# Token-major linear layers: four chunks of 256 columns, one token tile at a time, become chunks of 512 columns over all token tiles at once

## The chip, the cores and the metric

One core of a Trainium2 chip runs the whole program. Its engines are TensorE (PE, with its weight loads shown as PEld), VectorE (DVE), ScalarE (ACT), GpSimd (POOL) and SyncE (SP, which issues most DMAs). PE writes its results to PSUM, here eight banks of 128x512 float32. The metric is the device time of one execution in microseconds (us); the lower the better.

## What is computed

Two transformer blocks on 512 tokens of width 1024, batch 1, in float32. What matters here are four linear layers whose output is wanted token by token (tokens on the partitions):

```
z = h @ w_in                        # mixer A: v columns (512) of [u, gate, q, k, v, f]
z = h @ w_in                        # mixer B: v columns (512) of the dilated heads, 128 of the sliding heads
k, v = split(mem_n @ w_kv, 2)       # cross attention, in both layers: v, 256 memory tokens x 1024
... = h @ gdn_w_in                  # gated delta net: output gate z, 1024 columns; out = norm(o) * silu(z)
```

All other linear layers are wanted feature by feature and are not touched.

## The kernel before, in words

**Precision and pieces.** A float32 product is made of three fp32r matmuls (`mm3`): high x high, high x low, low x high part. Activations come as pairs `(high, low)` of tiles `xs[k]`, one for each of eight blocks k of 128 features. Weights come in pieces of 128x1024: a DMA into `ws`, a cast on ACT to `wh` (line 130), a subtraction on DVE for `wl` (line 131). `BUFS` gives 4 buffers to `ws` and 3 each to `wh` and `wl`. `wap` returns a generator over a chunk's pieces, so that a piece is asked for only when the loop comes to it.

**Token-major layers.** `lin_t` goes over chunks of 256 columns. For a chunk it takes the whole list of pieces (two, of four k each), and then for each tile of 128 tokens `lin_1` takes one PSUM bank of tag `lin`, runs 8 x 3 matmuls with the tokens as the stationary operand and 256 columns of weights moving (lines 152 to 154), and calls the evacuation. `lin_f` is the feature-major counterpart: weights stationary, 512 tokens moving.

**PSUM.** `BANKS = {"lin": 2, "pt": 1, "s": 3, "o": 2}`: eight banks with a tag each. `s` serves attention scores, the LRU's gates (lines 487, 488), and in the gated delta net (GDN) the decay matrices (lines 980 to 983), the transposes of X (line 1034), and in each level of the block inverse the products `pz` (line 1055), `px` (line 1062) and `py` (line 1065). DVE writes Z out of `pz` (line 1059), then subtracts `py` from Y (line 1067) and `px` from X (line 1069).

**Order.** The kernel is written with a library that places the instructions itself: a planner goes through them with the order of writing as their priority and its own estimates of durations. Whatever is ready and first in the order goes next into its engine's queue, so that later work fills an engine that would otherwise stand still. A tile takes a buffer of its tag when its first instruction is placed, and gives it back after its last reader. The queues are fixed when the kernel is built; on the chip each engine runs its queue in order and waits on semaphores.

**The sum of squares.** `rms_prep` makes the squares (ACT, line 202) and adds them on POOL (line 207). The rest, matmuls with ones (line 222), a reciprocal root on DVE (lines 224 to 242) and its broadcast (lines 251 to 254), is written at the first call of `rms()`, in most layers in the first evacuation.

**The sites.** In `ab` (evacuation line 381) the v layer stands before the LRU. In `cd` (line 545) it is the first layer, and its evacuation is the first to call `rms()`. In `xa_kv` (lines 657, 658: ACT writes the high part, DVE the low part) there are two tiles of tokens; the feature-major K layer stands before it. In `gdn` the z layer stands after four groups of two heads (lines 869, 870) and before the gating of all heads (lines 876 to 887): `sz` and the pairs `gy` take buffers of tag `x` (16), which `xs` and the groups' tiles hold until they are through.

Of the kernel before, what the change touches and what calls it, by code (L numbers as in the profile page):

```python
# [11 lines left out]
AF = mybir.ActivationFunctionType  # L12
OP = mybir.AluOpType
# [5 lines left out]
S = 512  # L19
D = 1024  # L20
NT = 4
# [12 lines left out]
class Kern:  # L34
# [129 lines left out]
    def lin_t(self, w, chunks, xs, evac, cols=256, N=S):  # L164

        for c in chunks:
            ws = list(w(c))
            for t in range(N // 128):
                self.lin_1(ws, t, xs, lambda p: evac(c, t, p), cols)

    def lin_1(self, ws, t, xs, evac, cols=256):
        p = self.psum("lin")[:, :cols]
# [192 lines left out]
    def ab(self):  # L365
        nc, A = self.nc, self.A
        V = VCOL
        vec = self.vec
        xs, rms = self.rms_prep(self.hT, V["ab_norm"])
        w = self.wap("ab_w", 8, 128)  # L370
        ahead = lambda c: self.early.pop(0) if self.early else w(c)
        fx, c = self.t("fx")[:8], self.t("c")[:8]
        u, g = self.tiles("u", 4), []
        v = self.tiles("v", 4, "x")
# [3 lines left out]
            nc.vector.tensor_tensor(y, p, rms()[1], op=OP.mult)  # L378

        def ev_v(c, t, p):  # L380
            nc.scalar.activation(v[t][:, c * 256:(c + 1) * 256], p, AF.Copy, scale=rms()[0][:, t:t + 1])

        self.lin_f(ahead, [0], xs, lambda n, p: nc.vector.tensor_tensor(fx, p, rms()[1][:8], op=OP.mult), cols=8)

# [9 lines left out]
        lw = self.tconst("lruw")  # L394
        self.lruw, self.lruw2 = lw[:, :S], lw[:, S:]
        uc = self.conv4(u, V["conv_w"], V["conv_b"])
        self.lin_t(self.wap("ab_wv", 8, 256), range(2), xs, ev_v)
        self.lru(uc)
        g += self.tiles("g", 4)
        self.lin_f(w, range(12, 16), xs, ev)  # L400
# [123 lines left out]
    def cd(self):  # L524
        nc, V = self.nc, VCOL
        xs, rms = self.rms_prep(self.hT, V["cd_norm"])
        C, Sn = self.pair("CS")
        w = self.wap("cd_w", 8, 128)

        def rotated(p, scale):  # L530
            z, zr, y = self.t("z"), self.t("zr"), self.t("qk")
            nc.scalar.activation(z, p, AF.Copy, scale=scale)
            for a, b in ((0, 32), (32, 0), (64, 96), (96, 64)):
                nc.sync.dma_start(zr[a:a + 32], z[b:b + 32])
            nc.gpsimd.tensor_tensor(zr, zr, Sn, op=OP.mult)
            nc.vector.tensor_tensor(z, z, C, op=OP.mult)
            nc.vector.tensor_tensor(y, z, zr, op=OP.add)
            return y

        v = self.tiles("v", 4, "x")  # L540
        vd_ = self.t("vd")
        vd = [vd_[:, t * 128:(t + 1) * 128] for t in range(NT)]

        def ev_v(c, t, p):
            nc.scalar.activation(v[t][:, c * 256:(c + 1) * 256] if c < 2 else vd[t], p, AF.Copy, scale=rms()[0][:, t:t + 1])

        self.lin_t(self.wap("cd_wv", 8, 256), range(2), xs, ev_v)
        self.lin_t(self.wap("cd_wvd", 8, 128, -2), [2], xs, ev_v, cols=128)
        nc.vector.tensor_tensor(C, self.cos, rms()[1], op=OP.mult)
        nc.vector.tensor_tensor(Sn, self.sin, rms()[1], op=OP.mult)  # L550
        ys = [self.pair("y", "y", F32R) for _ in range(4)]
        qp, kp = [None] * 8, [None] * 5

        def proj_q(i, n):
            def ev(n, p):
                qp[i] = self.q_parts(rotated(p, -0.125))
            self.lin_f(w, [n], xs, ev)

        def proj_k(i, n):
            def ev(n, p):  # L560
                kp[i] = self.k_parts(rotated(p, 1.0))
            self.lin_f(w, [n], xs, ev)

        def dilated(i):
            mn, den = self.small((128, 8), "mn"), self.small((128, 8), "den")
            o = self.psum("pt")
            for j in range(8):
                qb, e = NT - 1 - j // 2, j % 2
                h, nk, qs = 2 * i + e, (qb + 1) * 128, slice(qb * 128, (qb + 1) * 128)
                P = self.probs(self.qk(qp[i], *kp[i], e, qs, slice(0, nk)), nk, self.dstrip[:, 512 - nk:],  # L570
                               mn[:, j:j + 1], den[:, j:j + 1])
                self.pv(o[:, j * 64:(j + 1) * 64], P, nk, [v[b][:, h * 64:(h + 1) * 64] for b in range(qb + 1)])
            self.pair_out(self.o_norm(o, den, 8), ys[i])

        def sliding(i):

            mn, den = self.small((128, 8), "mn"), self.small((128, 8), "den")
            o = self.psum("pt")
            for j in range(8):
                qb, e = NT - 1 - j // 2, j % 2  # L580
                h, k0, qs = i + 4 * e, max(0, qb - 1) * 128, slice(qb * 128, (qb + 1) * 128)
                nk = (qb + 1) * 128 - k0
                P = self.probs(self.qk(qp[4 + i], *kp[4], e, qs, slice(k0, k0 + nk)), nk, self.sstrip[:, 256 - nk:],
                               mn[:, j:j + 1], den[:, j:j + 1], floor=self.nsink[:, h:h + 1])
                self.pv(o[:, j * 64:(j + 1) * 64], P, nk,
                        [vd[k0 // 128 + b][:, e * 64:e * 64 + 64] for b in range(nk // 128)])
            x = self.small((128, 8), "es")
            sinks = self.nsink.rearrange("p (e i) -> p i e", e=2)[:, i]
            nc.vector.tensor_tensor(x.rearrange("p (t e) -> p t e", e=2), mn.rearrange("p (t e) -> p t e", e=2),
                                    sinks[:, None].to_broadcast([128, NT, 2]), op=OP.subtract)  # L590
            nc.scalar.activation(x, x, AF.Exp)
            nc.vector.tensor_tensor(den, den, x, op=OP.add)
            ys.append(self.rpair("y"))
            self.pair_out(self.o_norm(o, den, 8), ys[4 + i])

        def proj(i):
            if i < 4:
                proj_k(i, 4 + i)
                proj_q(i, i)
            elif i < 8:  # L600
                if i == 4:
                    proj_k(4, 12)
                proj_q(i, 4 + i)

        proj(0)
        for i in range(8):
            proj(i + 1)
            if i == 6:
                self.mem_load()
            if i == 7:  # L610
                self.xa_kv(1)
            (dilated if i < 4 else sliding)(i % 4)
        for j in range(8):
            self.dump("d_y2", rd(ys[j][0]), lambda o: o[j])
        self.lin_f(self.wap("cd_wo", 8, 128), range(8), ys, self.add_resid)
# [22 lines left out]
    def xa_kv(self, l):  # L638
        nc, V = self.nc, VCOL
        rcol, rbc = self.mem_r  # L640
        xs = []
        for k in range(8):
            if k % 2 == 0:
                h2, m2 = self.rpair("mx")
            c = slice((k % 2) * 256, (k % 2 + 1) * 256)
# [7 lines left out]
        vv = [[self.T("xv", "y", F32R) for _ in range(2)] for _ in range(2)]  # L653

        def ev_v(c, t, p):
            (h, m), r, c = vv[t], rcol[:, t:t + 1], slice(c * 256, (c + 1) * 256)
            nc.scalar.activation(h[:, c], p, AF.Copy, scale=r)
            nc.vector.scalar_tensor_tensor(m[:, c], p, r, rd(h[:, c]), op0=OP.mult, op1=OP.subtract)

        self.lin_f(self.wap("xa_wk", 8, 128, 8 * l), range(8), xs, lambda n, p: nc.vector.tensor_tensor(kT[n], p, rbc, op=OP.mult), N=256)  # L660
        self.lin_t(self.wap("xa_wv", 8, 256, 4 * l), range(4), xs, ev_v, N=256)
        self.xkv = (kT, vv)

    def xa(self, l):
# [121 lines left out]
    def gdn(self):  # L786
# [76 lines left out]
        sz = []  # L863

        def ev_z(c, t, p):
            if t == 0:
                sz.append(self.T("sz", "x").rearrange("p (n i c) -> p n i c", n=NT, i=2))
            th, z = self.t("zt", tag="P")[:, :256], sz[c].rearrange("p n i c -> p n (i c)")[:, t]
            nc.scalar.activation(th, p, AF.Tanh, scale=hr[:, t:t + 1])
            nc.vector.scalar_tensor_tensor(z, th, 1.0, p, op0=OP.add, op1=OP.mult)  # L870

        self.lin_t(self.wap("gdn_wz", 8, 256), range(4), xs, ev_z)
        ys = self.ys = [self.rpair("gy") for _ in range(8)]
        for grp in range(4):
            o, rs = ot[grp]
# [1030 lines left out]
def chunks(w, cols):  # L1906

    k, n = w.shape
    return np.ascontiguousarray(w.reshape(k // 128, 128, n // cols, cols).transpose(2, 1, 0, 3)).reshape(n // cols, 128, -1)


def layout(I):
    f = np.float32
    A = {}
# [17 lines left out]
    w = I["ab_w_in"][0]  # L1932
    u, g, q, k, v, fl = np.split(w, [512, 1024, 1536, 2048, 2560], axis=1)
    A["ab_w"] = chunks(np.concatenate([u, q, k, g], 1), 128)
    A["ab_wv"] = chunks(v, 256)
    A["ab_wf"] = chunks(fl, 8)
    A["ab_wo"] = chunks(I["ab_w_out"][0], 128)
    bd = np.zeros((2, 4, 128, 128), f)
# [6 lines left out]
    qc, kc, vc, qd, kd, vd = np.split(w, [512, 1024, 1536, 2048, 2176], axis=1)  # L1945
    qd = qd.reshape(D, 2, 4, 64).transpose(0, 2, 1, 3).reshape(D, 512)
    A["cd_w"] = chunks(np.concatenate([qc, kc, qd, kd], 1), 128)
    A["cd_wv"] = chunks(vc, 256)
    A["cd_wvd"] = chunks(vd, 128)
    wo = I["cd_w_out"][0]  # L1950
    A["cd_wo"] = chunks(np.concatenate([wo[:512], wo[512:].reshape(2, 4, 64, D).transpose(1, 0, 2, 3).reshape(512, D)]), 128)
    A["sink"] = np.ascontiguousarray(I["cd_sink"].reshape(1, 8))
    A["xa_wq"] = np.concatenate([chunks(I["xa_w_q"][l], 128) for l in range(2)])
    A["xa_wk"] = np.concatenate([chunks(I["xa_w_kv"][l][:, :D], 128) for l in range(2)])
    A["xa_wv"] = np.concatenate([chunks(I["xa_w_kv"][l][:, D:], 256) for l in range(2)])
    A["xa_wo"] = np.concatenate([chunks(I["xa_w_o"][l], 128) for l in range(2)])
    A["mlp_wu"] = np.concatenate([chunks(I["mlp_w_up"][l], 128) for l in range(2)])
    A["mlp_wd"] = np.concatenate([chunks(I["mlp_w_down"][l][g * 1024:(g + 1) * 1024], 128) for l in range(2) for g in range(4)])
# [14 lines left out]
    w = I["gdn_w_in_2"][0]  # L1973
    q, k, v, z = (w[:, i * 1024:(i + 1) * 1024] for i in range(4))
    A["gdn_w"] = chunks(np.concatenate([x[:, g * 256:(g + 1) * 256] for g in range(4) for x in (k, q, v)], 1), 128)
    A["gdn_wz"] = chunks(z, 256)
    A["gdn_wab"] = chunks(w[:, 4096:], 16)
    A["gdn_conv"] = I["gdn_conv_w_2"][0].reshape(4, 24, 128).transpose(2, 1, 0).reshape(128, 96)
    A["gdn_dt"], A["gdn_alog"], A["gdn_nw"] = I["gdn_dt_bias_2"], I["gdn_a_log_2"], I["gdn_norm_w_2"].reshape(128, 1)
# [63 lines left out]
```

## Time and profile before

| | |
|---|---|
| median of 3 runs | 2798.21 us (2798.03 to 2803.38) |
| the profiled execution's own time | 2798.65 us |
| its span in the trace | 2796.9 us |
| PE, PEld busy | 2682.8 us (96%), 2294.2 us (82%) |
| DVE, ACT, POOL busy | 1770.3 us (63%), 1367.6 us (49%), 181.9 us (7%) |
| DMA | 332.58 MB, mean 119 GB/s |

The span is what the trace covers; the time of the execution is a little longer. Busy shares are of the span. Matmuls overlap in PE's pipeline, so a matmul's duration in the trace is longer than the distance to the next one's start. The five places that are touched lie at about 50 to 79 us (`ab`), 223 to 246 (cross attention of layer 0), 757 to 785 (`cd`), 963 to 986 (cross attention of layer 1) and 1741 to 1837 (GDN).

### The profile page before, as it was taken

To read this page: it belongs to the slowest core of one execution; us is meant where nothing else is said; L and a number is where in the kernel's file an instruction comes from. 1 tells how busy PE (TensorE), PEld (TensorE's weight loads), DVE (VectorE), ACT (ScalarE), POOL (GpSimd) and SP (SyncE) were. 2 spreads that over 40 slices of the span, in tenths; PEclk is the share of its full clock that TensorE was granted. 3 is DMA by queue.
4 is the path that set the end of the run, shared out by engine and by line. 5 is a ranking of instruction groups with operands and counts; after the bars stand their busy time and mean duration, and the time that the engine had idled before them with its cause. 6 is when DMAs were issued, how large, how long until landed. Compare 5 with 4: busy or idle time off the path is not lost. (4 is left out here: it accounts for less than half of the span.)

```text
span 2796.9 us, 40163 instructions
## 1 busy us (share of the span) xinstructions
PE 2682.8 (96%) x15128; PEld 2294.2 (82%) x15128; DVE 1770.3 (63%) x3583; ACT 1367.6 (49%) x2541; POOL 181.9 (7%) x185
## 2 busy tenths in 40 slices
PE   8999999999999999999999999997997999997996
PEld 6889888888888888888887788997886888897885
DVE  6775564443447656535445877567878367667878
ACT  5654443332346544423334644335885255534885
POOL 1101010000111010100002000000001001000001
PEclk9999999999999999999999999998999999998998
DMA  4314233333333331334433222323887212013985
GB/s 138 100 41 148 70 94 92 97 98 98 91 86 92 106 106 42 109 98 127 149 94 128 85 71 63 93 69 129 303 291 275 91 42 73 24 45 100 313 295 190
DMA packets 122534, 332.58 MB, mean 119 GB/s; under 512 B 21716, under 2 KB 37748, under 8 KB 122328
## 3 DMA queue, kind: packets, MB, share of 16 engines
q1 hardware_dynamic: 119896, 321.43, 36.4%
q0 software_dynamic: 2432, 8.46, 0.8%
q8 instruction: 123, 2.02, 0.3%
q14 instruction: 83, 0.68, 0.1%
HBM read 301.49 MB, written 28.02 MB: 118 GB/s over the span
## 5 line engine op out<-in xcount | busy, mean ns | idle before, releaser
L130 ACT ACTIVATE wh<-ws 128x1024 fp32r<-128x1024 f32 (+2 forms) x521 | 534.1, 1030 | 828.8 <-PE lin L153 594.8
L131 DVE TENSOR_TENSOR wl<-ws,wh 128x1024 fp32r<-128x1024 f32 (+2 forms) x521 | 616.6, 1192 | 154.8 <-ACT wh L130 152.5
L152 PE MATMUL lin<-xs,wh 128*128 128x512 f32 (+2 forms) x1080 | 428.3, 397 | 7.4 <-ACT xs L197 5.9
L153 PE MATMUL lin<-xs,wh 128*128 128x512 f32 (+2 forms) x1080 | 429.0, 397 | 2.6 <-DVE xs L198 2.4
L154 PE MATMUL lin<-xs,wl 128*128 128x512 f32 (+2 forms) x1080 | 427.7, 396 | 0.9 <-DVE wl L131 0.9
L152 PEld LDWEIGHTS lin<-xs,wh 128*128 128x128 f32 (+2 forms) x1080 | 202.9, 188 | 50.9 <-ACT xs L197 6.8
L153 PEld LDWEIGHTS lin<-xs,wh 128*128 128x128 f32 (+2 forms) x1080 | 203.0, 188 | 47.6 <-DVE xs L198 7.1
L154 PEld LDWEIGHTS lin<-xs,wl 128*128 128x128 f32 (+2 forms) x1080 | 203.0, 188 | 42.3 <-DVE wl L131 1.4
L347 DVE TENSOR_TENSOR h<-lin,h 128x512 f32<-128x512 f32 x112 | 77.4, 691 | 247.6 <-PE lin L154 247.5
L152 PE MATMUL lin<-sr,wh 128*128 128x512 f32 x512 | 199.2, 389 | 0.0
L153 PE MATMUL lin<-sr,wh 128*128 128x512 f32 x512 | 199.2, 389 | 0.0
L154 PE MATMUL lin<-sr,wl 128*128 128x512 f32 x512 | 199.2, 389 | 0.0
L734 DVE SCALAR_TENSOR_TENSOR ra<-lin,bc 128x512 f32<-128x512 f32 x64 | 44.3, 692 | 168.5 <-PE lin L154 165.9
L305 ACT ACTIVATE P<-s,mn 128x256 f32<-128x256 f32 (+1 forms) x224 | 114.3, 514 | 52.7 <-DVE mn L303 50.1
L1539 PE MATMUL o<-oh,Rh 128*128 128x256 f32 x512 | 131.1, 292 | 5.6 <-PEq L1382 2.2
L1539 PE MATMUL o<-oh,Rl 128*128 128x256 f32 x512 | 130.0, 290 | 0.0
L152 PEld LDWEIGHTS lin<-sr,wh 128*128 128x128 f32 x512 | 96.1, 188 | 20.1
L154 PEld LDWEIGHTS lin<-sr,wl 128*128 128x128 f32 x512 | 96.1, 188 | 19.9
L153 PEld LDWEIGHTS lin<-sr,wh 128*128 128x128 f32 x512 | 96.1, 188 | 19.8
L153 PE MATMUL s<-wl,exh 128*128 128x512 f32 x256 | 105.1, 410 | 5.3 <-DVE wl L131 5.1
L313 PE MATMUL o<-c_ident,P 128*128 128x128 f32 x536 | 97.0, 282 | 12.2 <-ACT P L305 11.4
L1539 PEld LDWEIGHTS o<-oh,Rh 128*128 128x128 f32 x512 | 101.7, 199 | 8.6 <-ACT ex L1555 4.1
(605 smaller groups left out, 6174.4 us busy)
## 6 DMA issues: line engine op xcount, KB each, us to landing
ws<-in_moe_wgu SPq DMA_DIRECT2D x128, 512.0 KB, 5.9
ws<-in_mlp_wu SPq DMA_DIRECT2D x64, 512.0 KB, 3.6
ws<-in_mlp_wd SPq DMA_DIRECT2D x64, 512.0 KB, 3.6
ws<-in_moe_wd SPq DMA_DIRECT2D x64, 512.0 KB, 5.6
yd<-ey SPq DMA_DIRECT2D x56, 256.0 KB, 4.7
ws<-in_gdn_w SPq DMA_DIRECT2D x24, 512.0 KB, 3.7
ws<-in_ab_w SPq DMA_DIRECT2D x16, 512.0 KB, 4.4
ws<-in_xa_wk SPq DMA_DIRECT2D x16, 512.0 KB, 3.7
```

Of the source, the lines that this page charges most:

```text
L130: nc.scalar.activation(wh, ws, AF.Copy)
L131: nc.vector.tensor_tensor(wl, ws, rd(wh), op=OP.subtract)
L152: mm(out, a[0], b[0], start=start, stop=False)
L153: mm(out, a[0], b[1], start=False, stop=False)
L154: mm(out, a[1], b[0], start=False, stop=stop)
L305: nc.scalar.activation(P[:, :nk], p[:, :nk], AF.Exp, bias=mn, scale=-1.0, accum_out=den)
L313: nc.tensor.transpose(pt[:, b * 128:(b + 1) * 128], P[:, b * 128:(b + 1) * 128], self.ident)
L347: self.nc.vector.tensor_tensor(self.hT[n], p, self.hT[n], op=OP.add)
L734: nc.vector.scalar_tensor_tensor(a, p, 0.0, rms()[1], op0=OP.max, op1=OP.mult)
L1539: self.nc.tensor.matmul(p[:, j * 256:(j + 1) * 256], Rs[t][i][:, fs], oh[:, t], start=t + i == 0, stop=t == NT - 1 and i == 1)
```

## The change

A new function `lin_w` takes chunks of 512 columns. For a chunk it takes a PSUM tile for each tile of tokens, tagged `lin`, `lin`, `s`, `s` (only the first two in cross attention). It goes over the pieces of weights as they come (now two k each), and for each k over all tiles of tokens; after the last k it calls the evacuations of all tiles. Four layers call it in place of `lin_t`; the 128 columns of the sliding heads' v stay with `lin_t`. The evacuations work on 512 columns; that of z makes two `sz` tiles at a time and writes them with one DVE instruction each. The weights in DRAM are laid out in chunks of 512 columns.

```diff
+    def lin_w(self, w, chunks, xs, evac, N=S):
+
+        for c in chunks:
+            ps = [self.psum(tag) for tag in ("lin", "lin", "s", "s")[:N // 128]]
+            for k, b in w(c):
+                for t, p in enumerate(ps):
+                    self.mm3(p, tuple(x[:, t * 128:(t + 1) * 128] for x in xs[k]), b, k == 0, k == len(xs) - 1)
+            for t, p in enumerate(ps):
+                evac(c, t, p)
 
         def ev_v(c, t, p):
-            nc.scalar.activation(v[t][:, c * 256:(c + 1) * 256], p, AF.Copy, scale=rms()[0][:, t:t + 1])
+            nc.scalar.activation(v[t], p, AF.Copy, scale=rms()[0][:, t:t + 1])
...
-        self.lin_t(self.wap("ab_wv", 8, 256), range(2), xs, ev_v)
+        self.lin_w(self.wap("ab_wv", 8, 512), range(1), xs, ev_v)
...
-        self.lin_t(self.wap("cd_wv", 8, 256), range(2), xs, ev_v)
-        self.lin_t(self.wap("cd_wvd", 8, 128, -2), [2], xs, ev_v, cols=128)
+            nc.scalar.activation(vd[t] if c else v[t], p, AF.Copy, scale=rms()[0][:, t:t + 1])
+
+        self.lin_w(self.wap("cd_wv", 8, 512), range(1), xs, ev_v)
+        self.lin_t(self.wap("cd_wvd", 8, 128, -1), [1], xs, ev_v, cols=128)
...
-            (h, m), r, c = vv[t], rcol[:, t:t + 1], slice(c * 256, (c + 1) * 256)
+            (h, m), r, c = vv[t], rcol[:, t:t + 1], slice(c * 512, (c + 1) * 512)
             nc.scalar.activation(h[:, c], p, AF.Copy, scale=r)
             nc.vector.scalar_tensor_tensor(m[:, c], p, r, rd(h[:, c]), op0=OP.mult, op1=OP.subtract)
...
-        self.lin_t(self.wap("xa_wv", 8, 256, 4 * l), range(4), xs, ev_v, N=256)
+        self.lin_w(self.wap("xa_wv", 8, 512, 2 * l), range(2), xs, ev_v, N=256)
...
         def ev_z(c, t, p):
             if t == 0:
-                sz.append(self.T("sz", "x").rearrange("p (n i c) -> p n i c", n=NT, i=2))
-            th, z = self.t("zt", tag="P")[:, :256], sz[c].rearrange("p n i c -> p n (i c)")[:, t]
+                for _ in range(2):
+                    sz.append(self.T("sz", "x").rearrange("p (n i c) -> p n i c", n=NT, i=2))
+            th = self.t("zt", tag="P")
             nc.scalar.activation(th, p, AF.Tanh, scale=hr[:, t:t + 1])
-            nc.vector.scalar_tensor_tensor(z, th, 1.0, p, op0=OP.add, op1=OP.mult)
-
-        self.lin_t(self.wap("gdn_wz", 8, 256), range(4), xs, ev_z)
+            for i in range(2):
+                z, cs = sz[2 * c + i].rearrange("p n i c -> p n (i c)")[:, t], slice(i * 256, (i + 1) * 256)
+                nc.vector.scalar_tensor_tensor(z, th[:, cs], 1.0, p[:, cs], op0=OP.add, op1=OP.mult)
+
+        self.lin_w(self.wap("gdn_wz", 8, 512), range(2), xs, ev_z)
```

## Rows read from the trace of the kernel before

**Rows 1.** The page, part 1: busy us (share of the span) xinstructions of each engine.

```profile
PE 2682.8 (96%) x15128; PEld 2294.2 (82%) x15128; DVE 1770.3 (63%) x3583; ACT 1367.6 (49%) x2541; POOL 181.9 (7%) x185
```

**Rows 2.** Timeline of PE, cd: start us, us, engine, line, op, out<-in, shapes, count.

```profile
769.81 0.28 PE L152 MATMUL lin<-wh,xs 128*128 128x256 f32 x1
...
781.93 0.28 PE L154 MATMUL lin<-wh,xs 128*128 128x256 f32 x1
```

**Rows 3.** Timeline of PE, a feature-major layer of 512 columns.

```profile
399.61 0.39 PE L153 MATMUL lin<-y,wh 128*128 128x512 f32 x1
...
406.64 0.39 PE L154 MATMUL lin<-y,wl 128*128 128x512 f32 x1
```

**Rows 4.** Windows, cd and cross attention: stretch, length, each engine's busy us, PEclk, DMA.

```profile
757.00:797.00 40.00, 38.50 (x316) 37.58 (x315) 11.97 (x27) 12.91 (x21) 2.80 (x3) 1.00 0.23 70
960.00:990.00 30.00, 30.00 (x254) 29.82 (x253) 18.10 (x27) 16.11 (x26) 0.00 (x0) 1.00 0.58 175
```

**Rows 5.** Windows, instructions of tile xs alone: PE, PEld, DVE, ACT busy (count), PEclk.

```profile
1741.60:1769.60 28.00, 10.05 (x63) 8.12 (x63) 0.00 (x0) 0.00 (x0) 1.00 0.15 40
1769.60:1787.90 18.30, 15.95 (x131) 15.77 (x131) 0.00 (x0) 0.00 (x0) 1.00 0.34 97
1787.90:1797.60 9.70, 3.92 (x17) 3.42 (x17) 0.00 (x0) 0.00 (x0) 0.65 0.65 207
1797.60:1836.60 39.00, 25.89 (x174) 22.20 (x174) 0.00 (x0) 0.00 (x0) 1.00 0.25 82
```

**Rows 6.** Timeline of PE, GDN's last group; in brackets idle time before and its releaser.

```profile
1787.97 1.09 PE L1034 MATMUL s<-c_ident,X 128*128 128x128 f32 x8 [2.40 <-DMA X<-x]
...
1795.60 2.17 PE L1062 MATMUL s<-X,Z 128*128 128x64 f32 x16
1797.60 1.95 PE L1065 MATMUL s<-Z,X 128*128 128x64 f32 x16
...
1809.94 1.14 PE L1049 MATMUL s<-X,Z 64*64 64x64 f32 x16
```

**Rows 7.** Timeline of PE, the start of cd.

```profile
757.59 0.28 PE L152 MATMUL lin<-wh,xs 128*128 128x256 f32 x1
...
761.77 1.05 PE L222 MATMUL pt<-ones,ssq 128*128 128x1 f32 x8 [1.26 <-POOL ssq L207]
...
765.67 0.68 PE L252 MATMUL pt<-dg,ones 128*128 128x128 f32 x4 [0.23 <-DVE dg L251]
```

**Rows 8.** Timeline of DVE, the start of cd.

```profile
762.86 0.16 DVE L224 TENSOR_SCALAR ms<-pt 128x4 f32<-128x4 f32 x1 [2.26 <-PE pt L222]
...
765.04 0.16 DVE L242 SCALAR_TENSOR_TENSOR b<-u,b 128x4 f32<-128x4 f32 x1
```

**Rows 9.** Windows, GDN after the wait for X: all engines' busy us, PEclk, DMA.

```profile
1788.00:1796.00 8.00, 8.00 (x44) 8.00 (x44) 3.04 (x5) 0.60 (x1) 0.00 (x0) 0.58 0.64 192
```

**Rows 10.** Timeline of all engines, cross attention: a tile of tokens ends and is evacuated.

```profile
965.94 0.28 PE L154 MATMUL lin<-wh,mx 128*128 128x256 f32 x1
...
966.26 0.47 ACT L657 ACTIVATE xv<-lin,mem 128x256 fp32r<-128x256 f32 x1 [1.94 <-PE lin L154]
...
966.77 0.49 DVE L658 SCALAR_TENSOR_TENSOR xv<-lin,mem,xv 128x256 fp32r<-128x256 f32 x1 [1.19 <-ACT xv L657]
```

**Rows 11.** Groups by shape: count | busy us, mean ns of one | idle before.

```profile
L886 ACT ACTIVATE gy<-o,gdn_nw 128x512 fp32r<-128x512 f32 x8 | 5.4, 688 | 4.8 <-PE o L885 4.6
...
L1422 DVE SCALAR_TENSOR_TENSOR z<-yg,wh,z 128x512 f32<-128x512 f32 x16 | 11.1, 739 | 0.0
```

**Rows 12.** Timeline of DVE, GDN's last group.

```profile
1800.25 0.68 DVE L1069 TENSOR_TENSOR X<-X,s 128x512 f32<-128x512 f32 x1
...
1835.32 0.17 DVE L876 TENSOR_TENSOR b<-b,rcol 128x8 f32<-128x8 f32 x1
```

More of the change, by code (lines that the diff above doesn't have):

```diff
@@ L544, in ev_v @@
         def ev_v(c, t, p):
-            nc.scalar.activation(v[t][:, c * 256:(c + 1) * 256] if c < 2 else vd[t], p, AF.Copy, scale=rms()[0][:, t:t + 1])
-        self.lin_t(self.wap("cd_wv", 8, 256), range(2), xs, ev_v)
-        self.lin_t(self.wap("cd_wvd", 8, 128, -2), [2], xs, ev_v, cols=128)
+            nc.scalar.activation(vd[t] if c else v[t], p, AF.Copy, scale=rms()[0][:, t:t + 1])
+        self.lin_w(self.wap("cd_wv", 8, 512), range(1), xs, ev_v)
+        self.lin_t(self.wap("cd_wvd", 8, 128, -1), [1], xs, ev_v, cols=128)
         nc.vector.tensor_tensor(C, self.cos, rms()[1], op=OP.mult)
@@ L1934, in layout @@
     A["ab_w"] = chunks(np.concatenate([u, q, k, g], 1), 128)
-    A["ab_wv"] = chunks(v, 256)
+    A["ab_wv"] = chunks(v, 512)
     A["ab_wf"] = chunks(fl, 8)
@@ L1947, in layout @@
     A["cd_w"] = chunks(np.concatenate([qc, kc, qd, kd], 1), 128)
-    A["cd_wv"] = chunks(vc, 256)
+    A["cd_wv"] = chunks(vc, 512)
     A["cd_wvd"] = chunks(vd, 128)
@@ L1954, in layout @@
     A["xa_wk"] = np.concatenate([chunks(I["xa_w_kv"][l][:, :D], 128) for l in range(2)])
-    A["xa_wv"] = np.concatenate([chunks(I["xa_w_kv"][l][:, D:], 256) for l in range(2)])
+    A["xa_wv"] = np.concatenate([chunks(I["xa_w_kv"][l][:, D:], 512) for l in range(2)])
     A["xa_wo"] = np.concatenate([chunks(I["xa_w_o"][l], 128) for l in range(2)])
@@ L1975, in layout @@
     A["gdn_w"] = chunks(np.concatenate([x[:, g * 256:(g + 1) * 256] for g in range(4) for x in (k, q, v)], 1), 128)
-    A["gdn_wz"] = chunks(z, 256)
+    A["gdn_wz"] = chunks(z, 512)
     A["gdn_wab"] = chunks(w[:, 4096:], 16)
```

## The prediction

> **What bounds the kernel now.** I read the page's busy times first: TensorE (PE) is busy 96% of the span [rows 1], so a gap on PE is nearly always lost time, and 1% of PE work is worth about as much time. Then I looked at how fast PE runs its two kinds of matmul. In the layers that the change touches, 102 matmuls of 256 columns start 12.12 us apart from first to last, 0.1200 us each [rows 2]. In the layers of 512 columns, 32 start over 7.03 us, 0.2268 us each [rows 3]. So a 512-column matmul is 0.0132 us cheaper than two of 256. Last I looked at each of the five call sites for what keeps PE busy and what it waits for. In the V projection of cross attention PE has no gap at all; at the start of `cd` it is busy 38.5 of 40 us [rows 4]; in the gated delta net (GDN) the z projection fills the holes of a long chain [rows 5, 6].
>
> **Removed: half the matmuls, and their overhead.** The counts follow from the loops (three matmuls per tile of tokens, k and chunk). `ab_wv`: 2 chunks x 4 tiles x 8 x 3 = 192 of 256 columns; `cd_wv`: 192; `xa_wv`: two layers of 4 x 2 x 24 = 192 each; `gdn_wz`: 4 x 4 x 24 = 384. Together 1152 become 576 of 512 columns: 576 x 0.0132 = 7.6 us less PE work (1.3 in `ab`, 1.3 in `cd`, 2.5 in both cross attentions, 2.5 in GDN). Pieces of weights stay 128x1024, so their DMAs, their casts and their number are the same, at the same rate.
> The rows leave 13 ns of overhead on each matmul beyond its columns at 2.4 GHz. The Trainium skill (TensorE: Matmul & The Clock Gate, Back-to-back issue gap) gives columns/2.4 + 2.5 ns for an isolated pair of matmuls; by it the pair would save 2.5 ns, estimated 1.4 us in all. The rows measure five times that, and I use them.
>
> **ab.** The v chunk holds two of the three `s` banks for some 22 us, and the LRU's matmuls need two at a time. They are not on the path: their result is needed only after attention. The next user of `lin` finds its bank: tile 0 ends 9 matmuls (2.0 us) before the chunk does, and its evacuation takes about 0.7. So -1.3 us.
>
> **cd: the sum of squares comes later.** `rms()` runs its PE and DVE work when an evacuation first asks for it. Before, that was after tile 0's 24 matmuls: PE waited 1.26 us for the last `ssq` and ran L222, and while DVE made the reciprocal root, from 762.86 to 765.2, PE ran on with tile 1 [rows 7, 8]. After, the first evacuation stands behind all 96 matmuls of the chunk. All four accumulators are then full, none can be emptied before the root is there, and the next layer needs a `lin` bank. What covered the DVE chain is gone: PE is idle from L222's end (762.82 in the old times) to L252 at 765.67, 2.85 us [rows 7]. Gained are the old stalls, 1.26 + 0.23 [rows 7], since 84 matmuls (19 us) can run before the eighth k is needed.
> The idle time has a second price. After the one gap of 2.4 us in GDN the granted clock read 0.58 (a mix of its two levels) over the next 8 us [rows 6, 9]: 8 x 0.42 = 3.4 us of PE time; after the 1.26 us in `cd` it stayed at 1.00 [rows 4]. 2.85 is nearer the first, so I take 3.4 (bounds 0 and 3.4). `cd`: -1.3 - 1.5 + 2.85 + 3.4 = +3.5 us.
>
> **Cross attention: both lin banks at once.** With two tiles of tokens the chunk takes both `lin` banks, and its tiles end only three matmuls apart. Before, one bank emptied while the other filled: ACT starts 0.04 us after a tile's last matmul ends, DVE 0.04 after ACT [rows 10], and PE never waited [rows 4]. After, ACT and DVE work on 512 columns, 0.69 and 0.74 us by the like instructions [rows 11]. Tile 0's last matmul runs 0.39 us from its start [rows 3], so its bank is free 0.39 + 0.04 + 0.69 + 0.04 + 0.74 + 0.05 = 1.95 us after that start, where PE wants it 4 x 0.227 = 0.91 us after. That is 1.04 us of idle PE, once between the two chunks and once before the layer that follows, in two layers: 4.2 us. In layer 1 a few steps of the last sliding head can fill, so I take 3.2 (bounds 0, if other work always fills, and 4.2, or 1 us more each if a cast stands in front). Net -2.5 + 3.2 = +0.7.
> The Trainium skill (Perfetto Trace Analysis, Matmuls) says independent groups should rotate through different banks so that emptying one overlaps the next group's matmuls; that speaks against this loop, and the sum above is its price here.
>
> **GDN: the filler takes banks that the chain needs.** This is the large term. Before, z needs only `lin`, which the chain of group 3 doesn't use. The planner places single matmuls of z wherever PE would stand still: 62 of the 384 before 1769.6 (the row has 63, one is group 3's last), 131 up to 1787.9 while the block inverse goes through DRAM, 17 up to 1797.6, and 174 more up to 1836.6 [rows 5]. After, tiles 2 and 3 of each chunk sit in two of the three `s` banks until the chunk is done and evacuated. The inverse's levels need a bank for `px` and another for `py` at once: L1069 empties `px` only after L1065 has read X and written `py`. With one bank left `py` waits for the end of the z chunk.
> How long? z is 192 x 0.2268 = 43.5 us. Up to the arrival of X PE has run 193 x 0.120 = 23.2 us of it, and I let it do as much after; if one `s` bank slows group 3's decay stage, z gains on PE what the chain loses. So 20.3 us are left, the second chunk, with its banks taken. Some 2.0 more run before L1065 [rows 5]. Then the remaining 18.3 us run in one stretch while the chain stands, plus 1.0 for the evacuation of a bank and 0.9 for Y's two halves through one bank: `py` is 20.2 us late. From L1065 (1797.60) to the last scale (L876, 1835.32) [rows 6, 12] the chain takes its own time, with no z to fill it. It gives back 1.3 us, as z no longer ends at 1836.6, behind the chain, and some PE work of afterwards can move into the gaps: z's end frees the `x` slots for six of eight heads' gating, 24 transposes and 36 matmuls of the first two output tiles, about 2.2 + 4.3 = 6.5 us. Net +12.4 us, its own 2.5 of saved matmuls included. Bounds: -2.5, if the chain always gets its banks, and +20, if nothing moves in.
>
> **Sum.** -1.3 + 3.5 + 0.7 + 12.4 = +15.3 us on the profiled execution's 2798.65 (span 2796.9): 2813.9, and the median of the runs shown lies 0.4 below that execution: **2813.5 us**, slower by 0.5%.
>
> **Rivals.** A measurement of this kernel can tell about 0.2% (5.6 us) from no change.
> (1) Faster: the work of filling is placed around the chain, so that GDN keeps its -2.5, and the sum of squares is placed inside `cd`'s chunk, where PE has the operand since 761.7. Then -7.6 - 1.5 + 3.2 = -5.9, 2792.3 us (2789 if the cross attention's waits are filled as well). For it: the planner already mixes single matmuls finely. Against it: in `cd` L222 stood behind tile 0's matmuls, in the order of writing, and while `py` is blocked z is the only work that is ready. It decides if `py` is under 3 us late. Chance 0.15.
> (2) No change: `py` finds its bank, the rest as above: -1.3 + 3.5 + 0.7 - 2.5 = +0.4, 2798.6. It holds if the z chunk is nearly through when X arrives, or takes its `s` banks late. Chance 0.24.
> (3) Slower by another way: banks of a tag are given out in the order of writing. Then z's tiles 2 and 3 wait for the last `px` of group 3 (L1049, 1809.94) [rows 6]; until then only tiles 0 and 1 run, through three pieces of weights, 36 matmuls or 8.2 us. 35.3 us of z are left, where before 143 x 0.12 = 17.2 were: +18, in all +21, 2819. Chance 0.11.
> My forecast (`py` blocked, 2803 to 2823 with the bounds of its terms): 0.50.
>
> **Chances and range.** Faster 0.15, same 0.25, slower 0.60. The likeliest time is 2813. For 8 in 10 the range must reach over rival (2) and the edge of rival (1) below and over rival (3) and a second loss of clock above: 2794 to 2828.
>
> **What would show it.** In the new trace: 512-column matmuls of `wh,xs` starting every 0.227 us; in `cd` L222 after 96 matmuls, a gap of about 2.9 us after it and a clock below 1 behind that; between the two `xa_wv` chunks gaps of about 1 us that end on L658; in GDN an L1062 followed by a run of z matmuls, then L1065 some 20 us later than before, and PE gaps up to the last scale. The forecast is wrong if L1065 follows L1062 at once, if L222 sits inside the chunk, or if the PE gaps at those four places add up to less than 8 us.

## The result: 44 us slower, and where the time went

The changed kernel takes 2842.26 us (median of 4 runs, 2841.41 to 2848.9) against 2798.12 for the kernel before (4 runs, 2796.59 to 2803.38): a ratio of 1.0168, with a 95% interval of 1.0151 to 1.0184. Slower was forecast, by a third of this. The page of the changed kernel, busy times and granted clock by slices:

```profile
PE 2706.7 (95%) x14552; PEld 2289.7 (81%) x14552; DVE 1770.4 (62%) x3575; ACT 1360.9 (48%) x2517; POOL 181.9 (6%) x185
...
PEclk9999999999989999999999999698999999998998
```

PE has 576 matmuls fewer than in [rows 1] and is busy 23.9 us longer. Wider matmuls cannot do that; the clock line tells how: its slice 26 of 40 reads 6, and the mean granted clock fell from 0.982 to 0.968.

To find the places I matched the same instruction in both traces and took the difference of its starts (us; the last column names such pairs, before and after). In this kernel's numbering lines stand 10 or 11 lower down behind `lin_w` (L207 is now L217, L222 is now L232), 12 or 13 in GDN (L1034 is now L1047, the last px L1049 is now L1062), and up to 4 lower still in the experiments.

| stretch | forecast | measured | starts before, after |
|---|---|---|---|
| ab | -1.3 | +0.5 | 222.89, 223.39 |
| V layer, cross attention 0 | +0.8 | +1.2 | 252.08, 253.82 |
| start of cd | +3.5 | +12.9 | 752.15, 753.83 and 838.06, 852.62 |
| rest of cd, V layer 1 | -0.1 | +1.8 | 1038.07, 1054.43 |
| GDN's second group | 0 | +3.0 | 1655.82, 1672.31 and 1692.18, 1711.69 |
| GDN's last group with z | +12.4 | +24.2 | 1767.16, 1787.41 and 1862.08, 1906.52 |
| everything else | 0 | +0.4 | spans 2796.9, 2840.9 |

The 0.8 and -0.1 are the forecast's +0.7 split over the two layers. Two rows hold more than their layer. Of ab's +0.5, -0.6 lies ahead of the layer, in the start of the kernel, where nothing was changed: from the pair at 49.49 (48.89 after) to the pair at 104.18 (104.90), with the V layer and the LRU between them, ab costs +1.3. And V layer 1 by itself, from 963.06 (980.47) to 999.99 (1016.35), comes out 1.05 below the kernel before; the +2.85 ahead of it is the rest of cd, 1.5 of it beside a granted clock of 0.50 from 949.7 to 960.0, where the kernel before had 0.50 for 3.4 us.

**GDN.** PE's timeline of the last group after the change:

```profile
1789.52 0.47 PE L154 MATMUL lin<-wh,xs 128*128 128x512 f32 x1
1804.01 1.97 PE L1047 MATMUL s<-c_ident,X 128*128 128x128 f32 x8 [14.01 <-DMA X<-x]
...
1833.35 1.96 PE L1062 MATMUL s<-X,Z 64*64 64x64 f32 x16 [0.68 <-ACT Z L1059]
1835.24 0.79 PE L152 MATMUL s<-wh,xs 128*128 128x512 f32 x1
...
1882.76 0.39 PE L152 MATMUL lin<-wh,gy 128*128 128x256 f32 x1 [0.38 <-ACT gy L899]
```

and windows over it (stretch, length, busy time and count of PE, PEld, DVE, ACT, POOL, granted clock, DMA):

```profile
1780.00:1788.00 8.00, 8.00 (x55) 6.93 (x54) 4.84 (x15) 3.94 (x16) 0.00 (x0) 1.00 0.22 66
1788.00:1796.00 8.00, 2.00 (x11) 1.29 (x9) 5.80 (x24) 1.24 (x6) 0.00 (x0) 0.80 0.09 8
1796.00:1804.00 8.00, 0.00 (x0) 0.00 (x0) 1.32 (x2) 0.00 (x0) 0.00 (x0) 0.50 0.41 118
1804.00:1812.00 8.00, 7.14 (x32) 6.66 (x32) 1.38 (x2) 0.60 (x1) 0.00 (x0) 0.50 0.23 89
...
1836.00:1844.00 8.00, 8.00 (x40) 6.84 (x38) 2.35 (x8) 2.34 (x8) 0.00 (x0) 0.71 0.01 3
```

z starts with its tiles 0 and 1, in `lin`. After 36 matmuls, three pieces of weights times 12, nothing more of it runs, and PE stands 14.01 us for X, where the kernel before stood 2.40 [rows 6]. No `s<-wh,xs`, which is z's tiles 2 and 3, starts before 1835.24, right behind the last px, although from a matmul at 1783.04 up to X's arrival at 1804.01 nothing is written to an `s` bank. Nor is the chain's `py` (L1078) blocked: it starts at 1813.86, right behind `px` (L1075, 1810.40). So it is rival (3), not the forecast: z does not take the chain's banks, it waits behind the chain for them. The difference of 24 us in its parts: X comes 16.0 us later, against a lag of 20.2 at the pair where the table's stretch begins (-4.2). From X to the last px the chain takes 29.34 us instead of 21.97, at a clock of 0.50 (+7.4). From there to the first matmul of the output projection (`lin<-wh,gy`, 1882.76; 1838.86 before) it is 49.4 us instead of 28.9 (+20.5): 156 matmuls of z are left, 156 x 0.2268 = 35.4 us, where 143 x 0.120 = 17.2 were (+18.2), and the clock of 0.71 from 1836 to 1844 is worth about the other 2.3 (an estimate, 8 x 0.29); the missing 0.5 comes behind that matmul.

**cd.** PE behind the v chunk, and DVE in the gap:

```profile
781.20 0.95 PE L232 MATMUL pt<-ones,ssq 128*128 128x1 f32 x8
786.01 1.19 PE L262 MATMUL pt<-dg,ones 128*128 128x128 f32 x4 [3.86 <-DVE dg L261]
```

```profile
783.18 0.16 DVE L252 SCALAR_TENSOR_TENSOR b<-u,b 128x4 f32<-128x4 f32 x1
783.26 1.22 DVE L131 TENSOR_TENSOR wl<-ws,wh 128x1024 fp32r<-128x1024 f32 x1
784.40 0.15 DVE L250 TENSOR_TENSOR u<-b 128x4 f32<-128x4 f32 x1
```

```profile
782.00:790.00 8.00, 4.14 (x21) 4.05 (x20) 5.05 (x20) 3.48 (x6) 0.00 (x0) 0.74 0.25 68
790.00:798.00 8.00, 8.00 (x39) 8.00 (x40) 0.34 (x1) 0.37 (x1) 0.00 (x0) 0.50 0.00 0
798.00:806.00 8.00, 8.00 (x40) 8.00 (x39) 0.00 (x0) 0.73 (x2) 0.00 (x0) 0.50 0.00 0
806.00:814.00 8.00, 8.00 (x27) 6.81 (x28) 1.23 (x1) 1.31 (x2) 0.00 (x0) 0.55 0.21 57
814.00:822.00 8.00, 8.00 (x37) 6.62 (x36) 1.44 (x2) 1.96 (x3) 0.17 (x1) 1.00 0.26 52
```

The gap is where it was forecast, 3.86 us instead of 2.85, because a weight cast of 1.22 us got between the steps of the root on DVE. What was not forecast is how long the clock stays down: 0.50 for the whole layer of 128 columns that follows (788.03 to 808.34, 20.3 us; before it took 10.7, 784.57 to 795.24), and back only some 4.8 us into the next one.

**Cross attention 0 and ab.** PE's gaps, and windows of ab:

```profile
235.43 0.50 PE L152 MATMUL lin<-wh,mx 128*128 128x512 f32 x1 [0.89 <-DVE xv L668]
...
247.53 0.50 PE L152 MATMUL lin<-y,wh 128*128 128x512 f32 x1 [0.89 <-DVE xv L668]
```

```profile
96.72 0.50 PE L152 MATMUL lin<-xs,wh 128*128 128x512 f32 x1 [2.14 <-ACT wh L130]
```

```profile
72.00:80.00 8.00, 8.00 (x25) 4.28 (x24) 4.59 (x7) 7.95 (x11) 0.00 (x0) 1.00 0.25 68
80.00:88.00 8.00, 8.00 (x35) 6.22 (x34) 6.18 (x9) 7.92 (x11) 0.00 (x0) 1.00 0.08 19
88.00:96.00 8.00, 6.58 (x30) 5.10 (x28) 7.09 (x13) 7.91 (x10) 0.00 (x0) 1.00 0.30 96
```

The two waits for `lin` banks are there. In ab ACT (fourth busy column) is full for 24 us with the LRU's work, which now all comes behind the chunk; the cast of a weight piece stands behind it, and PE waits 2.14 us for that.

### The profile page after: what moved, and what is told of

Its sections match the earlier page's. It is cut to its first block, busy times and chain, and to the rows that moved or that the text cites. A ratio compares the mean times of both kernels' runs of the same rounds, so it can differ in the third digit from the quotient of the medians.

```text
span 2840.9 us, 38980 instructions
## 1 busy us (share of the span) xinstructions
PE 2706.7 (95%) x14552; PEld 2289.7 (81%) x14552; DVE 1770.4 (62%) x3575; ACT 1360.9 (48%) x2517; POOL 181.9 (6%) x185
```

## The experiments

Unless said otherwise each is one edit of the changed kernel (2842.26 us). The kernel before took 2796.2 to 2797.9 us beside them.

### GDN: what stops z

**z_old.** `gdn_wz` back to `lin_t` with chunks of 256.

> The changed kernel with z of GDN put back to chunks of 256 columns, tile by tile (the other four sites stay changed). Theory (in GDN the changed loop stops filling: z's tiles 2 and 3 stand until the last px of group 3, tiles 0 and 1 run dry after 36 matmuls, PE stands 14 us for X and the chain then runs at a granted clock of 0.50): all of it goes, the wait for X is filled, GDN comes out as in the kernel before, and the time falls by the 25 us that GDN lost: 2817 us, 3 more or less by clock falls after short gaps elsewhere. Rival (part of GDN's loss has another source, such as the fall of the clock at 1684 to 1692 ahead of z, or the order of group 3): 2822 us or more.

Measured 2812.65 us: 29.6 less, more than GDN's loss, because in this trace the clock also did not fall behind X (a gap of 2.78 us) nor in the second group. X to the last px took 18.84 us. The last group comes out 2.7 us below the kernel before, so its loss is z's loop.

**z_two.** Two tiles of tokens at a time, in the `lin` banks alone:

```
-self.lin_w(self.wap("gdn_wz", 8, 512), range(2), xs, ev_z)
+wz = self.wap("gdn_wz", 8, 512)
+for c in range(2):
+    for t0 in (0, 2):
+        half = [tuple(x[:, t0 * 128:t0 * 128 + 256] for x in k) for k in xs]
+        self.lin_w(wz, [c], half, lambda c, t, p: ev_z(c, t0 + t, p), N=256)
```

> The changed kernel with z of GDN in chunks of 512 columns, but two tiles of tokens at a time in the two lin banks; each piece of weights is fetched and cast twice (8 pieces more: 8 x 1.06 us on ACT, 8 x 1.22 us on DVE). Theory (it is the s banks that stop z): with lin banks alone z fills the wait for X as before, no gap of 14 us, clock 1.00 through the inverse's levels, and the wider matmuls save their 2.5 us: GDN at -2 to 0 against the kernel before, 2842.3 - 25 - 2 = 2815 us. Rival 1 (the weights' pieces stop z, whichever bank): z stops after 36 matmuls again, about 2842. Rival 2 (the casts that are done twice cost the chain on DVE, which is busy 6.9 to 7.8 of 8 us from 1768 to 1784): X comes some 5 to 10 us later than in the kernel before and the time is 2820 to 2827.

Measured 2823.67 us. z fills again (127 of its matmuls run before X, against 36), so the `s` banks stop it, and rival 1 falls. Rival 2 holds: PE's waits are now short,

```profile
1807.52 0.47 PE L152 MATMUL lin<-wh,xs 128*128 128x512 f32 x1 [1.76 <-ACT wh L130]
...
1815.74 0.33 PE L1051 MATMUL s<-c_ident,X 128*128 128x128 f32 x1 [0.93 <-DMA X<-x]
```

but X comes 6 to 7 us later than in the kernel before (1815.74 against 1787.97, less the lag of 21 to 22 us with which this GDN began), behind casts that are done twice. From z's first matmul to X, instructions of tile `wl` alone (PE, PEld, DVE, clock), in the kernel before and here:

```profile
1741.70:1787.90 46.20, 18.44 (x65) 12.22 (x64) 4.87 (x4) 1.00 0.23 63
```

```profile
1762.30:1815.70 53.40, 16.75 (x43) 7.90 (x42) 13.42 (x11) 1.00 0.41 118
```

DVE makes 11 of these casts instead of 4, 8.6 us more, and X takes 7.2 us longer. From the pair at 1692.18 (1712.61 here) to the one at 1862.08 (1885.82) this GDN loses 3.3 us to the kernel before, where the changed kernel loses 24.9.

**z_o.** z's tiles 2 and 3 in the two `o` banks: `tags=("lin", "lin", "o", "o")`.

> The changed kernel with one edit: z's tiles 2 and 3 take the two o banks instead of two s banks. Theory (banks of a tag go out in the order of writing): the o banks stand empty while the chain waits for X, but group 3's last steps, written ahead of z, use them up to 1854.6; z stops after 36 matmuls as before, PE stands about 14 us for X, and tiles 2 and 3 start only behind the last o of group 3, some 20 us later than in the changed kernel, in which 45 matmuls of z (10 us) ran between those last steps: about 2852 us. Rival (a bank goes to whoever is ready first, and z lost the s banks to the chain's own use): with the o banks empty z goes on through the wait for X, the 14 us gap and the half clock behind it go, and the time is 2816 to 2825.

Measured 2852.68 us, to a microsecond what the order of writing gives. The `o` banks stand empty just as the `s` banks did, and PE stands as long:

```profile
1798.53 0.47 PE L1047 MATMUL s<-c_ident,X 128*128 128x128 f32 x1 [14.02 <-DMA X<-x]
```

z's tile 2 comes 25 us behind the last px (1827.87), between the last steps that use `o`:

```profile
1853.15 0.79 PE L152 MATMUL o<-wh,xs 128*128 128x512 f32 x1
```

From the last px to the first matmul of the output projection it is now 65.0 us instead of 49.4. A bank that is empty goes to the chain if the chain's use of it is written first. This settles the point on which my forecast failed.

**z_dummy.** What the clock costs alone:

```
     self.mm3(p, ..., b, k == 0, k == len(xs) - 1)
+    if k == 5 and t == 1 and c == 0:
+        for _ in range(idle):            # 60 for z, 0 elsewhere
+            self.nc.tensor.matmul(p, self.grows[:, :128], b[0], start=False, stop=False)
```

> The changed kernel with 60 matmuls of 512 columns added that multiply zeros and add nothing to z's second accumulator, behind the 36th matmul of z, where z stops for want of a bank; everything else as in the changed kernel. They fill the wait of 14 us for X (60 x 0.227 = 13.6 us) and take nothing else away. Theory (a part of GDN's loss is the clock alone): the granted clock stays 1.00 into the inverse's levels, and from X's first transpose to the last px the chain takes about 22 us as in the kernel before instead of 29.3; the rest of z still stands behind it. 2842.3 - 7.4 = 2835 us. Rival (the levels are slow because no z matmuls run beside them, or by their own waits on DVE, not by the clock): the stretch keeps about 29 us and the time stays at 2841 to 2843.

The operand was not all zeros by then (each group writes to it), so these matmuls do add to one tile of z; PE's work is as stated. Measured 2834.38 us, 7.9 less. The gap before X shrank to 1.60 us and the levels began at full clock; midway, from 1810 on, behind one of the waits of 0.8 us that stand between the levels, the clock fell all the same:

```profile
1798.00:1806.00 8.00, 6.33 (x43) 5.01 (x41) 1.38 (x2) 0.60 (x1) 0.00 (x0) 1.00 0.55 193
1806.00:1814.00 8.00, 6.62 (x44) 6.29 (x43) 1.74 (x3) 0.00 (x0) 0.00 (x0) 0.75 0.19 66
1814.00:1822.00 8.00, 7.09 (x32) 6.90 (x32) 0.82 (x2) 0.00 (x0) 0.00 (x0) 0.50 0.19 68
```

X to the last px: 24.03 us, against 29.34 or 29.35 in all eight traces in which the gap of 14 us stood. So the clock is worth at least 5.3 us of the 7.4. The rest of the 7.9 is mostly the second group, where the clock did not fall this time (3.0).

### cd: the late root, and the clock behind it

**cd_early.** `rms()` is called on a line of its own ahead of `lin_w(... "cd_wv" ...)`.

> The changed kernel with one edit: cd asks for its reciprocal root before the v chunk instead of at the chunk's first evacuation. Theory (late root): in the changed kernel PE stands 3.86 us behind L232 and then runs at a granted clock of 0.50 to 812.6; both come from the root being asked for behind 96 matmuls. With the root asked for first, L232 and the broadcast stand among the first matmuls of the chunk, no gap is left behind the chunk, the clock stays 1.00, and cd costs -1.3 (fewer, wider matmuls) -1.5 (old stalls) against the kernel before, instead of +13.7: about 2842.3 - 16.5 = 2825.8 us, 2829 if the old stalls stay. Rival (the loop itself): four open accumulators or the stream of weight pieces make the chunk slow, wherever the root stands; then cd stays near +13.7 and the time near 2842.

Measured 2830.48 us. The start of cd, by the pairs of the table, comes out 2.0 us below the kernel before, 15 us less than in the changed one. The old stall stays, since L232 now stands behind 12 matmuls only, and nothing follows it:

```profile
763.45 1.05 PE L232 MATMUL pt<-ones,ssq 128*128 128x1 f32 x8 [1.09 <-POOL ssq L217]
```

```profile
782.00:790.00 8.00, 8.00 (x60) 7.46 (x58) 1.40 (x2) 4.04 (x6) 0.00 (x0) 1.00 0.26 84
```

The loop is not what is slow. The median lies 1.5 us above the 2829 that was forecast with the old stall: GDN's last group cost 24 us again, and the layers behind GDN some 6 us more, by falls of the clock.

**cd_vdlate.** The layer of 128 columns moved behind `proj(0)`.

> The changed kernel with one edit: in cd the 128-column layer (cd_wvd) is written behind the first two projections of 512 columns, instead of right behind the v chunk. The gap behind the chunk stays (about 3.9 us). Theory (the clock comes back with the kind of work): in the changed kernel the clock read 0.50 through the whole 128-column layer and came back 4.3 us into the 512-column layer behind it; with 512-column work straight behind the gap it comes back within 4 to 8 us, so that some 28 us at half clock become 4 to 8 us plus what the gap takes, worth about 10 us: 2832 us. Rival (a fixed time after a gap of that length): the clock stays at 0.50 for about 28 us whatever follows, and the time stays within 1 us of 2842.

```profile
788.00:792.00 4.00, 3.42 (x12) 3.22 (x13) 1.45 (x6) 2.75 (x5) 0.00 (x0) 0.50 0.44 135
792.00:796.00 4.00, 4.00 (x15) 3.19 (x15) 1.01 (x2) 0.27 (x1) 0.00 (x0) 0.79 0.00 0
796.00:800.00 4.00, 4.00 (x20) 3.30 (x19) 1.23 (x1) 1.55 (x2) 0.00 (x0) 1.00 0.00 0
...
812.00:816.00 4.00, 2.25 (x11) 2.06 (x10) 1.99 (x3) 1.24 (x2) 2.82 (x3) 0.50 0.00 0
...
820.00:824.00 4.00, 4.00 (x15) 3.52 (x15) 0.78 (x1) 1.31 (x2) 0.00 (x0) 0.50 0.00 0
824.00:828.00 4.00, 4.00 (x18) 3.27 (x17) 0.45 (x1) 0.00 (x0) 0.00 (x0) 0.95 0.46 131
```

Measured 2838.28 us (2835.98 to 2849.72): the mechanism was right, the gain was not. Behind the same gap of 3.86 us (it ends at 788.58) the clock is back by 796, after some 7 us at 0.50 instead of 27, so it is not a fixed time. But the moved layer met two new waits for ACT (1.40 and 2.21 us, ahead of 809.74 and 816.46), the clock fell again and stayed at 0.50 through the rest of that layer.

### Cross attention: both lin banks at once

**xa_alt.** Each layer's second chunk in two `s` banks: `self.lin_w(wv, [1], xs, ev_v, N=256, tags=("s", "s"))`.

> The changed kernel with one edit: the second of the two V chunks of cross attention takes two s banks, the first the two lin banks as before. Theory (both lin banks full at once): the two waits of 0.89 us on L668 in layer 0 go, because the second chunk starts in empty banks and the layer behind it finds the lin banks empty; layer 0 comes out 1.3 us below the kernel before instead of 1.1 above. In layer 1 the two stalls are already filled by the last sliding heads, whose steps need s banks themselves; at best nothing changes, at worst those steps come late by a chunk (11 us) with nothing lost on PE. About 2842.3 - 2.4 = 2839.9 us. Rival (the evacuations are the limit, 0.69 us on ACT and 0.74 us on DVE for each tile with casts in between, whichever bank): the waits move behind the second chunk and less than 1 us is won.

Measured 2834.27 us. In layer 0 both waits are gone,

```profile
235.13 0.39 PE L152 MATMUL s<-wh,mx 128*128 128x512 f32 x1
...
246.01 0.39 PE L152 MATMUL lin<-y,wh 128*128 128x512 f32 x1
```

and it comes out 1.2 us below the kernel before instead of 1.2 above, as forecast. In layer 1 it costs: from 963.06 (977.24 here) to 999.99 (1015.34) it is 1.2 us above the kernel before, where the changed kernel is 1.05 below, with the sliding heads' steps now behind the chunk. The rest of the 8 us is falls of the clock that this trace lacks (3.0 in GDN's second group, others behind GDN).

### ab: not the banks

**ab_o.** v's tiles 2 and 3 in the `o` banks.

> The changed kernel with one edit: in ab the v chunk's tiles 2 and 3 take the two o banks instead of two s banks. Theory (late LRU): in the changed kernel the LRU's second matmul stands until 71.8 us for an s bank, its ACT work piles up at 73 to 96 us with ACT busy 7.9 of 8 us, the casts of the next weight pieces stand behind it, and PE waits 2.14 us at 96.7. With the LRU's banks free, L498 follows L497 at once, the wait goes, and ab comes out 1.3 to 2.5 us below the kernel before instead of 0.5 above: about 2840 us. Rival (the four evacuations of 512 columns and the weight stream make ACT late by themselves): the wait at 96 us stays and the time stays within 0.5 us of 2842.3.

Measured 2839.72 us, but the theory falls: L498 starts at 72.57 us, behind the whole chunk, with two `s` banks empty, the wait is the same, and from 49.49 to 104.18 ab costs +2.3, with a fall of the clock behind the wait:

```profile
97.50 0.60 PE L152 MATMUL lin<-xs,wh 128*128 128x512 f32 x1 [2.15 <-ACT wh L130]
```

**ab_lru.** `self.lru(uc)` written ahead of the v chunk.

> The changed kernel with one edit: in ab the LRU's steps are written ahead of the v chunk instead of behind it. With the o banks for v's tiles the LRU's second matmul had still stood behind the whole chunk (72.57 us) and PE had waited 2.15 us for the cast of a weight piece, so it was not the banks. Theory (order of work): the LRU is only placed where v has nothing ready; before, the two lin banks and the pieces left a hole at 52.8 us in which two of its four channel tiles ran, now there is none, all of its ACT work comes behind the chunk, and the casts queue behind it. With the LRU written first its ACT work runs beside the chunk, ACT is not full at 73 to 96 us, the wait of 2.1 us goes, and ab comes out 1.3 to 2.5 us below the kernel before: 2839.5 to 2841 us. Rival (the work of ACT is the same and only moves): PE waits about as long for a cast at another place, 2842, or for the LRU's own operands in the first part of the chunk, up to 2845.

Measured 2848.31 us; from 49.49 to 104.18 ab costs +5.0. The rival is right: ACT is full earlier, and PE waits for a cast there (2.69 us at 75.88, then 0.94).

```profile
64.00:72.00 8.00, 8.00 (x37) 6.61 (x36) 6.13 (x9) 7.92 (x9) 0.00 (x0) 1.00 0.01 2
72.00:80.00 8.00, 4.37 (x14) 2.67 (x13) 7.66 (x13) 6.22 (x8) 0.00 (x0) 0.77 0.03 10
```

**ab_half.** Two of the LRU's channel tiles ahead of the chunk, two behind:

```
     for j in range(4):
+        if j == 2:
+            mid()          # the v chunk
         pr, pi = self.psum("s"), self.psum("s")
```

> The changed kernel with one edit: in ab two of the LRU's four channel tiles are written ahead of the v chunk and two behind it. Written behind it (the changed kernel) all four come after the chunk, ACT is full from 73 to 96 us and PE waits 2.14 us for a cast; written ahead of it all four come first, ACT is full from 56 to 72 us and PE waits 2.69 + 0.94 us for casts. Theory (ACT is full for as long as the LRU's work comes in one piece, and the casts of the weights stand behind it): split in two, as the kernel before happened to do it, each piece fits between two casts, PE has no wait over 0.5 us in 48 to 105 us, and ab comes out 1.3 to 2.5 us below the kernel before, against 0.5 above in the changed kernel: about 2840 us, and 3 us less where the wait had brought the clock down as well. Rival (the v chunk itself, with its pieces and four evacuations, leaves ACT no room): a wait of 2 us or more stays.

Measured 2838.93 us. PE has no wait in 48 to 104 us and is busy 55.99 of 56. From 49.49 (47.89 here) to 104.18 (100.88) ab comes out 1.7 us below the kernel before, as forecast. The table's pair (222.89, here 219.38) reads 3.5 below, but 1.6 of that was there ahead of the layer; in the trace of best (below), whose ab is the old one, the same pair reads 2.4 below.

```profile
56.00:64.00 8.00, 8.00 (x37) 6.64 (x36) 7.79 (x11) 7.46 (x8) 0.00 (x0) 1.00 0.40 143
64.00:72.00 8.00, 8.00 (x37) 6.60 (x37) 3.99 (x4) 1.33 (x2) 0.00 (x0) 1.00 0.44 133
...
80.00:88.00 8.00, 8.00 (x37) 6.61 (x36) 6.32 (x13) 7.91 (x9) 0.00 (x0) 1.00 0.00 0
```

ab's cause is shown by the three together: not the banks, but the LRU's ACT work in one piece. The kernel before had it in two, through a hole in the v layer that the wider chunk closed: its LRU matmuls start at 52.83 to 56.50 and again at 76.84 to 81.05, and ACT is full behind each:

```profile
56.00:64.00 8.00, 8.00 (x61) 7.52 (x62) 6.29 (x9) 7.94 (x12) 0.00 (x0) 1.00 0.43 134
...
80.00:88.00 8.00, 7.99 (x34) 5.95 (x33) 4.62 (x8) 7.94 (x11) 0.00 (x0) 1.00 0.32 104
```

### A version from the parts that pay

**best.** The kernel before, with cd's wide chunk and the root asked for behind its fourth k, and cross attention's wide chunks (layer 0's second one in `s`); **best_half** has ab's wide chunk with the split LRU besides.

> The kernel before with the parts of the change that pay: cd's v chunk of 512 columns with the root asked for in the middle of the chunk (behind the fourth k), cross attention's chunks of 512 columns, layer 0's second one in two s banks, layer 1's both in the lin banks; ab and GDN as in the kernel before. Expected from the parts: cd -1.3 -1.5, layer 0 -1.2, layer 1 -1.0, together -5.0: 2793 us against 2798, a ratio of 0.998. Rival (the falls of the clock behind gaps of 1 to 2 us elsewhere, which come in one run and not in another, are as large as this gain): the ratio's interval contains 1.

> The kernel with the parts that pay (cd with the root asked for in the middle of the chunk, cross attention of 512 columns with layer 0's second chunk in s banks, GDN as before), and ab's v chunk of 512 columns with the LRU split in two around it, in place of the old ab. If the split takes the wait away: 1.3 to 2.5 us below the 2795.3 of the kernel without it, 2793 to 2794, ratio to the kernel before 0.998. If not: 2796 to 2798, ratio 0.999 to 1.000.

Measured 2795.3 us (11 runs) for best, a ratio of 0.999 (0.9981 to 0.9999), and 2792.37 us (12 runs) for best_half, 0.9985 (0.9975 to 0.9996). Both intervals lie below 1, but best misses its 2793 and the gain is about what such runs can tell. Places in the traces tell more: in best the start of cd comes out 2.3 us below the kernel before, layer 0 1.2 and V layer 1 1.0, and ab in best_half 1.7 (49.49 to 104.18). PE has no gap left at L234, which now stands behind 48 matmuls.

## Why the prediction was wrong

- **GDN: the step failed.** The forecast had "tiles 2 and 3 of each chunk sit in two of the three `s` banks" while the inverse needs them. The chain was never short of one, and z_o shows why: an empty bank waits for the use that is written first. That "a tile takes a buffer of its tag when its first instruction is placed", as the kernel's description has it, left this out. So +12.4 was the price of a wait that did not occur, and that the sign came out right is not the forecast's merit. Rival (3) had this mechanism at 0.11, with 36 matmuls of z and +18 behind the last px, both as counted in the trace (36, and 35.4 - 17.2 = 18.2). What it lacked was the half clock behind the 14 us gap (+7.4). The rows that spoke for rival (3) could not be read from the kernel before, where z never shares a bank with the chain.
- **cd: right mechanism, wrong size.** L222 behind 96 matmuls and the gap came as forecast (3.86 for 2.85). The term of 3.4 for the clock measured about 12 (12.9 + 1.3 + 1.5 - 3.86 = 11.8): 9.6 in the 128-column layer (20.3 - 10.7), the rest in the broadcasts before it and the first 512-column matmuls behind it. I had taken how long the fall lasts from a place with other work behind it [rows 9].
- **Cross attention: right in its mechanism.** In layer 0 1.04 was forecast for a wait, 0.89 came; from start to start they cost 1.15 and 1.21 (12.04 and 12.10 us for 48 matmuls, which are 10.89). Layer 1 filled both of its own (-1.05, where -0.1 was forecast with one of them). The Trainium skill (Perfetto Trace Analysis, Matmuls) has independent groups rotate through different banks; xa_alt agrees, with 2.4 us for layer 0.
- **ab: the step failed.** "They are not on the path: their result is needed only after attention" is true of the LRU's result, not of its ACT work, which stands ahead of casts that PE needs: a wait of 2.14 us, and +1.3 where -1.3 was forecast.
- **Matmuls: right.** In xa_alt 48 of 512 columns run from 235.13 to 246.01, 0.2267 us each, and its layer 0 gains the 1.2 us that the count gives.
- **Not forecast:** +3.0 in GDN's second group, by a fall of the clock behind a gap of 1.81 us that was 1.83 in the kernel before, with no fall. No part of the change is there. z_dummy and xa_alt, with gaps of 1.60 and 1.50, have no fall, z_two and best_half, with 1.57 and 1.51, have one; what decides it stays open.

## What to carry to other kernels

When filler work gets a resource in common with the chain it fills for, ask who was promised the resource first, not who is ready: if the chain was, the filler stops and the holes come back. A lazily computed operand should be asked for where other work is still open behind it. Price a gap on PE with what stands behind it, since the clock may stay down for all of that.

## What the runs showed of the hardware

- Behind the same gap of 3.86 us the granted clock read 0.50, its lower level, for about 27 us in the changed kernel, where a layer of 128-column matmuls follows, and for about 7 us in cd_vdlate, where 512-column ones follow. The Trainium skill (TensorE: Matmul & The Clock Gate, Part 1) says that activity releases the throttle; in the rows from 790 to 806 PE shows as busy 8.00 of 8.00 us and the granted clock stays at 0.50.
- The same short gap may or may not cost the clock. Behind ab's wait of 2.13 us in xa_alt and of 2.15 in ab_o:

```profile
97.40:101.40 4.00, 3.77 (x14) 2.52 (x15) 3.96 (x6) 1.83 (x2) 0.00 (x0) 1.00 0.33 73
```

```profile
97.50:101.50 4.00, 4.00 (x10) 2.67 (x11) 3.96 (x6) 1.84 (x2) 0.00 (x0) 0.57 0.27 95
```

  Of the nine traces with this wait four show the fall. X's wait of 2.40 us in the kernel before was followed by it, that of 2.78 in z_old was not. cd's gap of 3.86 us was followed by it in all ten traces that have it. Single runs of one kernel differ by several us (best from 2791.01 to 2797.93), so gains of 1 or 2 us were read from the place in the trace, not from the medians.
